# Adding the experts' results into x2 in place, with more weight tiles in rotation

## The chip, the core and the metric

The kernel runs on one core of a Trainium2 chip. The core has a matmul engine (TensorE, PE), a vector engine (VectorE, DVE), an activation engine (ScalarE, ACT), GpSimd (POOL) and SyncE (SP), which here only issues DMAs; 16 DMA engines move the data between DRAM and the on-chip memory (SBUF). Matmul results land in PSUM. The metric is the device time of one execution in microseconds (us); lower is better.

## What is computed

One decoder layer on 256 tokens of 2048 values, in float32. A mixer (pooling, sparse attention and cross-attention, gated) is projected by `w_o` and added to the input; the result is called x2 here. Behind it comes a mixture of experts (MoE) in which each token goes to two experts of one group of four:

```python
x = x + merged @ w_o
x = x + hierarchical_moe(rms_norm(x, g_ffn), ...)   # returned

def hierarchical_moe(h, ...):
    g_top = argmax(h @ w_router_group)               # one of 4 groups
    pe_top, e_local = top_k(softmax(le of g_top), 2) # 2 of its 4 experts
    a = einsum('bsd,edf->bsef', h, w_e_gate)         # 16 experts, 2048 x 512
    b = einsum('bsd,edf->bsef', h, w_e_up)
    act = silu(a) * b * combine[..., None]
    return einsum('bsef,efd->bsd', act, w_e_down)    # 512 x 2048
```

## The kernel before

The layer runs as one stream of matmuls. Up to about 620 us come the projections and the attention; from there to about 717 us the projection by `w_o`, in four chunks of 512 columns (n = 0 to 3), whose results DVE adds into x2 (L817, L820), an SBUF tile of 128 x 2 x 2048; then the routing; and from 731 us the MoE. In the projections every weight tile (`rawt`) is split into a high and a low part: ACT makes `wh` (L114), DVE the product of the difference, `wl` (L115), and PE multiplies with both (L268 to L270).

The MoE gathers its tokens with matmuls. For a group of four experts a 0/1 matrix `sel` says which token stands in which of the 64 places of each expert; `Gather.step` multiplies it with columns of x2 that `part` has split into high and low (ACT L915, DVE L916), and so fills `xg`. The group's four experts run as two pairs, 8 pairs in all. A pair takes 24 weight tiles of 1 MB: 8 for the gate, 8 for the up projection (matmuls `gu<-..,xg`) and 8 for the down projection (`dn<-..,aT`). `scatter` splits the down result into high and low (`ob`, ACT L1107, DVE L1108) and brings it back to token order by a matmul with the transposed `sel` (`selT`); DVE adds that to y (L1115), which for the first pair means x2 + result. In the last pair the rows go out by DMAs on ACT's queue (L1117). A loop behind the 8 pairs repeats them for experts with more than 64 tokens; with these inputs it runs zero times.

All weight tiles are loaded on SP's queue, in program order (`load`, L190). Their SBUF buffers come from what is dead by then, in the order of the deque `order`: 4 buffers of the first normed input (`hq`, tile name `wh`), NEX from a pool of their own (`ex`, `we`), 4 of the raw weights (`raw`, `wr`), and 4 of the merged mixer output (`mx0`, `mx1`, `wm`). `prefetch` takes the next tile of `todo` and the next buffer of `order`, and puts the buffer back at the end, except mx1: these two serve once and then become the accumulators y. Eighteen tiles are prefetched during the `w_o` phase (L733 ff., `pre`, and the `while` after it), and two more, `late`, are loaded after the routing's first part into buffers of a pool that is closed after the first pair. After that a tile is loaded as soon as the buffer that is next in `order` has been read for the last time, so 16 buffers rotate.

`wrt` holds the router's weights, 256 KB. It is loaded early by GpSimd (L356), scaled by DVE (L419) and read in the `w_o` phase (L800); then its memory holds the routing's intermediate tables. GpSimd's other DMAs bring x, biases (`bgt`) and small tables.

Of the kernel before, what the change touches and what calls it, by code (L numbers as in the profile page):

```python
# [20 lines left out]
P = 128  # L21
# [9 lines left out]
CAP = 64  # L31
NEX = 6
LOOK = 2
# [20 lines left out]
def layer_kernel(tc, x, xT, memT, pos, cst, band, gains, bgate, wmem, wxq, widx, wkqvp, wpg, wgb, wo, wr, we, out):  # L54
# [15 lines left out]
    def close(cm):  # L70
        cm.__exit__(None, None, None)

    c_c, cp = pool("const")
    c_raw, raw = pool("raw", bufs=4)
# [55 lines left out]
    big = cp.tile([P, NT, D], F32, tag="big", name="xin")  # L130
    wrt = cp.tile([P, KD, 32], F32, name="wrt")

    xin = big.rearrange("p t d -> p (t d)").rearrange("p (k s) -> p k s", s=S)
# [221 lines left out]

    tc.keep_in_program_order(nc.gpsimd.dma_start(wrt, wr))  # L356
    vm = tok(c4("vm"))
# [45 lines left out]
    def prep_tables():  # L403
        yield
        yield
        yield from tables(tabs)
        for nm, gi, sc in (("q", 0, scale), ("k", 1, 1.0)):
            if sc != 1.0:
                V.tensor_scalar(gn[:, gi], gn[:, gi], sc, None, op0=ALU.mult)
            g1 = gn[:, gi, 0:64].unsqueeze(1).to_broadcast([P, NT, 64])  # L410
            g2 = gn[:, gi, 64:128].unsqueeze(1).to_broadcast([P, NT, 64])
            tl = []
            for tt, (src, g) in enumerate((("cos", g1), ("sin", g2), ("cos", g2), ("sin", g1))):
                d = ap.tile([P, NT, 64], F32, name="tab%s%d" % (nm, tt))
                V.tensor_mul(d, tabs[src], g)
                tl.append(d)
            tabs[nm] = tl
            yield
        tc.keep_in_program_order(V.tensor_mul(wrt, wrt, cs[:, C_GFFN : C_GFFN + KD].unsqueeze(2).to_broadcast([P, KD, 32])))  # L419
        V.tensor_mul(gx, gn[:, 2], gn[:, 3])  # L420
        V.tensor_scalar(gx, gx, scale, None, op0=ALU.mult)
# [307 lines left out]
    todo = deque(use)  # L729
    late = [(0, 7), (0, 15)]  # L730
    for w in late:
        todo.remove(w)

    def prefetch():
        pr, i = todo.popleft()
        kind = order.popleft()
        if kind == "raw":
            w = raw.tile([P, 4, 512], F32, tag="raw", name="wr")
        elif kind == "hq":
            w = htp.tile([P, 4, 512], F32, tag="hq", name="wh")  # L740
        elif kind == "ex":
            w = pools["exp"][1].tile([P, 4, 512], F32, tag="ew", name="we")
        else:
            w = mgp.tile([P, 4, 512], F32, tag=kind, name="wm", bufs=2)
        if kind != "mx1":
            order.append(kind)
        if (pr, i) == (NE // 2 - 1, 23):
            load(w[:, 0:2], we[pr, i, :, 0:2])
            load(w[:, 2:4], we[pr, i, :, 2:4])
        else:  # L750
            load(w, we[pr, i])
        ahead.append(w)
# [29 lines left out]
    for t in range(NT):  # L782
        nc.gpsimd.dma_start(x2[:, t], x[t * P : (t + 1) * P, :])
    ss2 = cp.tile([P, NT, 4], F32, name="ss2")
    rps = sm_tile([P, S], "rps")
    rl_ = []

    def route_in(n, t, ac):
        owp = pools["ow"][1]
        sl = x2[:, t, n * 512 : (n + 1) * 512]  # L790
        ps = sm_tile([P, 4, P])
        for kk in range(4):
            nc.tensor.transpose(ps[:, kk], sl[:, kk * P : (kk + 1) * P], ident)
        xt = owp.tile([P, 4, P], F32, tag="xt", name="xt", bufs=2)
        A.activation(xt, ps, AF.Copy)
        A.activation(ac, sl, AF.Square, accum_out=ss2[:, t, n : n + 1])
        yield

        for kk in range(4):
            mm(rps[32 * kk : 32 * kk + 32, t * P : (t + 1) * P], wrt[:, 4 * n + kk], xt[:, kk],  # L800
               start=n == 0 and t == 0, stop=n == 2 and t == 1)
        yield
        if n == 2 and t == 1:
            lgT = owp.tile([P, 4, P], F32, tag="xt", name="lgT", bufs=2).rearrange("p a b -> p (a b)")[:, :S]
            V.tensor_copy(lgT, rps)
            yield
            rl_.append(sm_tile([P, NT, 20], "rl"))
            for u in range(NT):
                mm(rl_[0][:, u], lgT[:, u * P : (u + 1) * P], cs[:, C_SUM : C_SUM + 20], start=u == 0, stop=False)
            yield  # L810

    last = []
    for n in range(4):
# [9 lines left out]
        def pre(i, n=n):  # L823
            if n == 0 and i == 2:
                drain()
                close(c_cr)
                close(c_bt)
                pools["exp"] = pool("exp", bufs=NEX, side="left")
                pools["ow"] = pool("ow", side="right")
            if i % 2 == 1 and len(ahead) < 4 + NEX:  # L830
                prefetch()
# [29 lines left out]
    for t in range(NT):  # L861
        for kk in range(4):
            pe(rl[:, t], xts[t][:, kk], wrt[:, 12 + kk, 0:20], start=False, stop=t == 1 and kk == 3)
    for t in range(NT):
        pin(A.activation(last[t], x2[:, t, 3 * 512 :], AF.Square, accum_out=ss2[:, t, 3:4]))
    warm(14, ident, P, wps)
    close(pools["ow"][0])
    close(c_spl)
# [4 lines left out]
    pools["x"] = pool("early", side="right")  # L873
    for j, w in enumerate(late):
        et = pools["x"][1].tile([P, 4, 512], F32, name="we%d" % j)
        load(et, we[w])
        ahead.insert(use.index(w), et)

# [18 lines left out]
    C = [P, NT * 5, 4, 4]  # L897
    w = wrt.rearrange("p a b -> p (a b)")
    Rc = w[:, 0:40].rearrange("p (t e) -> p t e", e=4)
# [6 lines left out]

    def part(k, dve=False):

        xs = wk.tile([P, 2, NT, P], F32R, tag="xs", name="xs", bufs=3)
        src = x2[:, :, k * P : (k + 1) * P]  # L910
        if dve:
            pin(V.tensor_copy(xs[:, 0], src))
            pin(V.tensor_sub(xs[:, 1], src, xs[:, 0]))
        else:
            A.activation(xs[:, 0], src, AF.Copy)  # L915
            V.tensor_sub(xs[:, 1], src, xs[:, 0])  # L916
        return xs

    parts0 = [part(k, True) for k in range(3)]
    pin(V.tensor_copy(Rc, R.rearrange("p t g e -> p (t g) e")))  # L920
# [20 lines left out]
    class Gather:  # L941

        def __init__(self, q, slot_, parts=()):
            self.q = q
            self.sel = wk.tile([P, NT, EQ, 64], F32R, tag="sel", name="sel")
            for t in range(NT):
# [5 lines left out]
            self.flat = self.sel.rearrange("p t e s -> p t (e s)")  # L954
            self.xg = None
            self.parts = deque(parts)
# [3 lines left out]
        def split(self, n):  # L960
            while len(self.parts) < n and self.next < KD:
                self.parts.append(part(self.next))
                self.next += 1
# [17 lines left out]
        def back(self, wp):  # L981

            self.selT = wp.tile([P, 2, S], F32R, tag="selT", name="selT", bufs=2)
            ps = sm_tile([P, 2, NT, P])
# [19 lines left out]
    gf = cs[:, C_GFFN : C_GFFN + KD]  # L1004
    ga = Gather(0, slot, parts0)
    ga.step()
# [20 lines left out]

    cwf = rt([P, NT, 18], "cwf")
    cw = wk.tile([P, 2, NT, 18], F32R, name="cw")
# [4 lines left out]

    ys_ = []
    open_ = deque()
# [4 lines left out]

    def pair(pr, slot_, base, store, ga):
        hf = pr % 2
# [27 lines left out]
        else:  # L1071
# [4 lines left out]
            if hf == 0:  # L1076
                ga.factors()
            elif not store:
                nx = Gather(pr // 2 + 1, slot_)
                nx.split(3)  # L1080
# [19 lines left out]
        if nx is not ga:  # L1100
            nx.step()
        if not ys_:
            ys_.extend(mgp.tile([P, D], F32, tag="mx1", name="y", bufs=2) for _ in range(NT))

        def scatter(ad, c0, n):
            ob = w2.tile([P, 2, 512], F32R, tag="ob", name="ob", bufs=2)[:, :, :n]
            A.activation(ob[:, 0], ad, AF.Copy)  # L1107
            V.tensor_sub(ob[:, 1], ad, ob[:, 0])  # L1108
            yield
            for t in range(NT):  # L1110
                ps = sm_tile([P, 512])[:, :n]
                for u in range(2):
                    pe(ps, ga.selT[:, hf, t * P : (t + 1) * P], ob[:, u], start=u == 0, stop=u == 1)
                ys = ys_[t][:, c0 : c0 + n]
                V.tensor_add(ys, base(t)[:, c0 : c0 + n], ps)  # L1115
                if store:
# [41 lines left out]

    yb = lambda t: ys_[t]
    xb = lambda t: x2[:, t]  # L1160
    for pr in range(NE // 2):
        ga = pair(pr, slot, xb if pr == 0 else yb, pr == NE // 2 - 1, ga)
        if pr == 0:
            nri = rounds()


    reg = nc.values_load(nri[0:1, 0:1], min_val=0, max_val=S // CAP - 1)
    todo.extend(use)
    with tc.For_i(0, reg):
        V.tensor_scalar(slot, slot, -float(CAP), None, op0=ALU.add)  # L1170
        ga = Gather(0, slot)
        for pr in range(NE // 2):
            ga = pair(pr, slot, yb, pr == NE // 2 - 1, ga)

# [7 lines left out]
    close(c_raw)  # L1182
    close(c_c)


# [77 lines left out]
```

## Time and profile before

| | us |
|---|---|
| Median of 3 runs (lowest, highest) | 1191.76 (1190.85, 1193.13) |
| Profiled execution | 1192.13 |
| its span | 1190.4 |
| PE busy | 1150.9 |
| DVE busy | 575.2 |
| ACT busy | 424.6 |

The span is what the profile covers of the profiled execution; 1.7 us lie around it. The busy time of an engine is a sum over all stages, so a high share of it does not tell by itself what sets the end: that is read from stretches of the time line, from what an instruction waited for, and from the share in which the DMA engines moved data. HBM reads are 337 MB in all, 201 MB of which are the experts' weights.

### The profile page before, as it was taken

How to read it: one execution, taken by the hardware profiler on the slowest of the kernel's cores; microseconds unless marked ns; L12 is line 12 of the kernel's file. 1: busy time of each engine (PE TensorE's matmuls, PEld its weight loads, DVE VectorE, ACT ScalarE, POOL GpSimd, SP SyncE). 2: the span in 40 equal slices, each digit the busy share in tenths (PEclk: the TensorE clock that was granted, in tenths of full speed). 3: DMA queues.
4: the chain of work that ended last, by engine and by line, in shares of the span. 5: the costliest groups of instructions: out<-in, count | busy, mean ns of one | idle time of the engine just before them, and what ended most of it. 6: DMA issues, size and time to landing. Idle time of an engine off the chain costs nothing.

```text
span 1190.4 us, 14757 instructions
## 1 busy us (share of the span) xinstructions
PE 1150.9 (97%) x5879; PEld 789.1 (66%) x5879; DVE 575.2 (48%) x945; ACT 424.6 (36%) x661; POOL 30.2 (3%) x33
## 2 busy tenths in 40 slices
PE   8999999999999999999999998899999999899976
PEld 5788887888878888888887775454543634363423
DVE  7877468956455465465464444222321512050202
ACT  7765564446544444444444432201100301020000
POOL 4200000000000000000000000000000000000000
PEclk9999999999999999999999999999999999999998
DMA  9646545555546556565787567989999999999996
GB/s 385 208 140 234 184 150 177 177 177 181 202 177 200 206 191 213 189 206 210 252 348 300 188 226 280 384 297 426 426 426 426 427 425 426 426 426 426 426 426 244
DMA packets 49901, 340.34 MB, mean 286 GB/s; under 512 B 5664, under 2 KB 6304, under 8 KB 10400
## 3 DMA queue, kind: packets, MB, share of 16 engines
q1 hardware_dynamic: 46512, 329.83, 71.5%
q0 software_dynamic: 1728, 7.15, 1.7%
q10 hardware_dynamic: 1584, 2.34, 0.6%
q8 instruction: 48, 0.79, 0.3%
q14 instruction: 29, 0.24, 0.1%
HBM read 337.20 MB, written 2.10 MB: 285 GB/s over the span
## 4 chain that ended last, share of the span: by engine, by line


## 5 line engine op out<-in xcount | busy, mean ns | idle before, releaser
L115 DVE TENSOR_TENSOR wl<-rawt,wh 128x1024 fp32r<-128x1024 f32 (+1 forms) x240 | 292.3, 1220 | 212.7 <-ACT wh L114 211.8
L114 ACT ACTIVATE wh<-rawt 128x1024 fp32r<-128x1024 f32 (+1 forms) x240 | 251.0, 1048 | 298.3 <-PE acc L270 292.8
L269 PE MATMUL acc<-wl,hT 128*128 128x512 f32 (+1 forms) x640 | 249.7, 390 | 0.7 <-DVE wl L115 0.7
L270 PE MATMUL acc<-wh,hT 128*128 128x512 f32 (+1 forms) x640 | 247.3, 387 | 0.0
L268 PE MATMUL acc<-wh,hT 128*128 128x512 f32 (+1 forms) x640 | 228.5, 390 | 0.0
L269 PEld LDWEIGHTS acc<-wl,hT 128*128 128x128 f32 x640 | 120.2, 188 | 25.1 <-DVE wl L115 1.1
L270 PEld LDWEIGHTS acc<-wh,hT 128*128 128x128 f32 x640 | 120.2, 188 | 23.2
L268 PEld LDWEIGHTS acc<-wh,hT 128*128 128x128 f32 x640 | 119.2, 188 | 23.4 <-issue 0.3
L842 PE MATMUL gu<-we,xg 128*64 128x512 f32 x400 | 89.8, 596 | 1.5 <-DMA we<-in_we_dram 1.5
L842 PEld LDWEIGHTS gu<-we,xg 128*64 128x64 f32 x400 | 27.3, 137 | 54.2 <-issue 46.6
L842 PE MATMUL gu<-wh,xg 128*64 128x512 f32 x256 | 58.0, 596 | 4.4 <-DMA wh<-in_we_dram 4.4
L915 ACT ACTIVATE xs<-x 128x256 fp32r<-128x256 f32 x61 | 25.2, 416 | 97.4 <-PE sm L842 95.6
L1107 ACT ACTIVATE ob<-dn 128x512 fp32r<-128x512 f32 (+1 forms) x33 | 19.3, 585 | 111.8 <-PE dn L842 111.8
L842 PE MATMUL gu<-wr,xg 128*64 128x512 f32 x240 | 56.2, 596 | 3.0 <-DMA wr<-in_we_dram 3.0
L1108 DVE TENSOR_TENSOR ob<-dn,ob 128x512 fp32r<-128x512 f32 (+1 forms) x33 | 22.3, 676 | 68.7 <-ACT ob L1107 68.7
L1092 DVE SCALAR_TENSOR_TENSOR sgm<-sgm,fac,gu 128x512 f32<-128x512 f32 x8 | 6.0, 747 | 97.2 <-PE gu L842 97.1
L269 PE MATMUL acc<-wl,mgT 128*128 128x512 f32 x128 | 51.3, 401 | 0.0
L1115 DVE TENSOR_TENSOR y<-y,sm 128x512 f32<-128x512 f32 (+1 forms) x58 | 36.3, 665 | 30.5 <-PE sm L842 30.5
L270 PE MATMUL acc<-wh,mgT 128*128 128x512 f32 x128 | 50.7, 396 | 0.0
L268 PE MATMUL acc<-wh,mgT 128*128 128x512 f32 x128 | 46.7, 398 | 0.0
L842 PE MATMUL dn<-we,aT 128*64 128x256 f32 x384 | 46.1, 385 | 0.7 <-ACT aT L1099 0.7
L842 PEld LDWEIGHTS gu<-wh,xg 128*64 128x64 f32 x256 | 17.5, 137 | 42.5 <-issue 30.3
(343 smaller groups left out, 1320.1 us busy)
## 6 DMA issues: line engine op xcount, KB each, us to landing
we<-in_we_dram SPq DMA_DIRECT2D x74, 1024.0 KB, 19.5
rawt<-in_wgb_dram SPq DMA_DIRECT2D x64, 1024.0 KB, 4.8
wh<-in_we_dram SPq DMA_DIRECT2D x48, 1024.0 KB, 19.5
wr<-in_we_dram SPq DMA_DIRECT2D x45, 1024.0 KB, 19.4
rawt<-in_wkqvp_dram SPq DMA_DIRECT2D x24, 1024.0 KB, 4.9
wm<-in_we_dram SPq DMA_DIRECT2D x24, 1024.0 KB, 19.4
rawt<-in_wo_dram SPq DMA_DIRECT2D x16, 1024.0 KB, 4.8
rawt<-in_wmem_dram SPq DMA_DIRECT2D x7, 1024.0 KB, 8.3
```

Of the source, the lines that this page charges most:

```text
L114: pin(A.activation(hi, ps, AF.Copy))
L115: pin(V.tensor_sub(lo, ps, hi))
L268: mm(o, hi[:, c], wh[:, kk], start=f, stop=False)
L269: mm(o, hi[:, c], wl[:, kk], start=False, stop=False)
L270: mm(o, lo[:, c], wh[:, kk], start=False, stop=l)
L842: i = mm(*a, **k)
L915: A.activation(xs[:, 0], src, AF.Copy)
L1092: V.scalar_tensor_tensor(sg, sg, c1s, au, op0=ALU.mult, op1=ALU.mult)
L1107: A.activation(ob[:, 0], ad, AF.Copy)
L1108: V.tensor_sub(ob[:, 1], ad, ob[:, 0])
L1115: V.tensor_add(ys, base(t)[:, c0 : c0 + n], ps)
```

## The change

The experts' results are no longer collected in y. Each pair's results are added into x2 itself. A token belongs to one group only, so for the other groups' gathers an added row is not needed; the adds bring zeros to the rows of other groups. For the overflow loop, which gathers the original values again, x2 is stored to DRAM (`x0d`) before the MoE and would be read back there.

That frees mx1's two buffers, which now rotate. The router's weights get memory of a pool that lives only in the `w_o` phase, are loaded there and scaled there; the routing's tables lie in the not yet filled end of `xg`. selT and ob have one buffer instead of two, and the memory set aside for the descriptors of GpSimd's DMAs is 1024 (`dynamic_dma_scratch_size`). NEX is 9 instead of 6, and one tile is late instead of two: 21 buffers rotate instead of 16, and 22 tiles instead of 20 are issued before the MoE begins to give buffers back.

```diff
-NEX = 6
+NEX = 9
@@ layer_kernel
+    c_d, dp = pool("dram", space=bass.MemoryType.DRAM)
-    wrt = cp.tile([P, KD, 32], F32, name="wrt")
-    tc.keep_in_program_order(nc.gpsimd.dma_start(wrt, wr))
-        tc.keep_in_program_order(V.tensor_mul(wrt, wrt, cs[:, C_GFFN : C_GFFN + KD].unsqueeze(2).to_broadcast([P, KD, 32])))
@@ weight tiles
-    late = [(0, 7), (0, 15)]
-    for w in late:
-        todo.remove(w)
+    late = (0, 15)
+    todo.remove(late)
-        if kind != "mx1":
-            order.append(kind)
+        order.append(kind)
@@ pre(i), n == 0 and i == 2
+                wrt_.append(pools["ow"][1].tile([P, KD, 32], F32, name="wrt"))
+                nc.gpsimd.dma_start(wrt_[0], wr)
+                V.tensor_mul(wrt_[0], wrt_[0], cs[:, C_GFFN : C_GFFN + KD].unsqueeze(2).to_broadcast([P, KD, 32]))
@@ after the last add into x2
+    for t in range(NT):
+        load(x0d[t], x2[:, t])
-    for j, w in enumerate(late):
-        et = pools["x"][1].tile([P, 4, 512], F32, name="we%d" % j)
-        load(et, we[w])
-        ahead.insert(use.index(w), et)
+    et = pools["x"][1].tile([P, 4, 512], F32, name="we15")
+    load(et, we[late])
+    ahead.insert(use.index(late), et)
-    w = wrt.rearrange("p a b -> p (a b)")
+    xg0 = wk.tile([P, KD, 256], F32, tag="xg", name="xg")
+    w = xg0[:, 14:16].rearrange("p a b -> p (a b)")
@@ back, scatter
-            self.selT = wp.tile([P, 2, S], F32R, tag="selT", name="selT", bufs=2)
+            self.selT = wp.tile([P, 2, S], F32R, tag="selT", name="selT")
-            ob = w2.tile([P, 2, 512], F32R, tag="ob", name="ob", bufs=2)[:, :, :n]
+            ob = w2.tile([P, 2, 512], F32R, tag="ob", name="ob")[:, :, :n]
-                ys = ys_[t][:, c0 : c0 + n]
-                V.tensor_add(ys, base(t)[:, c0 : c0 + n], ps)
+                ys = x2[:, t, c0 : c0 + n]
+                V.tensor_add(ys, ys, ps)
@@ build
-    nc = _bacc.Bacc("TRN2", target_bir_lowering=False, num_devices=1)
+    nc = _bacc.Bacc("TRN2", target_bir_lowering=False, num_devices=1, dynamic_dma_scratch_size=1024)
```

On SP's queue, from the last tile prefetched in the `w_o` phase on, before (we_5626 and we_5628 are the late tiles, the four `wh` the first reissues):

```order
L190 DMA wm<-in_we_dram 128x2048
L190 DMA we_5626<-in_we_dram 128x2048
L190 DMA we_5628<-in_we_dram 128x2048
L190 DMA wh<-in_we_dram 128x2048 x4
L190 DMA we<-in_we_dram 128x2048 x6
L190 DMA wr<-in_we_dram 128x2048
L190 DMA wm<-in_we_dram 128x2048
L190 DMA wr<-in_we_dram 128x2048
L190 DMA wm<-in_we_dram 128x2048
L190 DMA wr<-in_we_dram 128x2048 x2
L190 DMA wh<-in_we_dram 128x2048 x4
```

The same place after:

```order
L190 DMA wm<-in_we_dram 128x2048
L190 DMA x0d<-x_4891 128x2048 x2
L190 DMA we_5637<-in_we_dram 128x2048
L190 DMA wh<-in_we_dram 128x2048 x4
L190 DMA we<-in_we_dram 128x2048 x9
L190 DMA wr<-in_we_dram 128x2048
L190 DMA wm<-in_we_dram 128x2048
L190 DMA wr<-in_we_dram 128x2048
L190 DMA wm<-in_we_dram 128x2048
L190 DMA wr<-in_we_dram 128x2048
```

The two stores of x2 stand where a late tile stood, and a round of the rotation has 21 tiles instead of 16.

On DVE, at the start of the `w_o` phase (sg is the gated mixer, wl the low part of a `w_o` tile), before:

```order
L773 TENSOR_TENSOR sg<-acc,sg 128x512 x2
L775 TENSOR_TENSOR sg<-sg 128x512 x2
L115 TENSOR_TENSOR wl<-rawt,wh 128x1024 x3
L115 TENSOR_TENSOR mgT_2930<-sm,mgT_2930 128x4x128 x2
L115 TENSOR_TENSOR wl<-rawt,wh 128x1024 x4
```

and after:

```order
L769 TENSOR_TENSOR sg<-acc,sg 128x512 x2
L771 TENSOR_TENSOR sg<-sg 128x512 x2
L116 TENSOR_TENSOR wl<-rawt,wh 128x1024
L830 TENSOR_TENSOR wrt<-wrt,cs 128x512
L116 TENSOR_TENSOR wl<-rawt,wh 128x1024 x2
L116 TENSOR_TENSOR mgT_2929<-sm,mgT_2929 128x4x128 x2
```

The scaling of wrt, which before stood far ahead, now stands between two of the wl products.

## Rows read from the trace of the kernel before

**Rows 1.** The page, busy us and share of each engine.

```profile
PE 1150.9 (97%) x5879; PEld 789.1 (66%) x5879; DVE 575.2 (48%) x945; ACT 424.6 (36%) x661; POOL 30.2 (3%) x33
```

**Rows 2.** The page's 40 slices, DMA engines' busy share in tenths.

```profile
DMA  9646545555546556565787567989999999999996
```

**Rows 3.** Windows: stretch, length, PE, PEld, DVE, ACT, POOL, PE clock, DMA share, GB/s.

```profile
644.00:674.00 30.00, 30.00 (x156) 23.27 (x155) 14.48 (x14) 15.04 (x22) 0.00 (x0) 1.00 0.56 199
720.00:726.00 6.00, 4.89 (x43) 4.70 (x43) 4.74 (x29) 1.16 (x4) 0.44 (x2) 1.00 0.99 377
726.00:735.00 9.00, 7.47 (x44) 4.43 (x45) 5.28 (x25) 3.13 (x7) 0.00 (x0) 1.00 0.26 87
765.00:810.00 45.00, 41.80 (x248) 19.67 (x246) 11.64 (x23) 5.72 (x9) 0.00 (x0) 0.96 0.81 313
840.00:1140.00 300.00, 288.50 (x1686) 134.39 (x1685) 78.99 (x151) 35.28 (x69) 0.00 (x0) 1.00 1.01 426
```

**Rows 4.** PE's time line (start, length), first gate matmuls of pairs 1 to 7.

```profile
791.85 1.94 PE L842 MATMUL gu<-we,xg 128*64 128x512 f32 x8
...
848.43 1.89 PE L842 MATMUL gu<-wr,xg 128*64 128x512 f32 x8
...
898.90 1.89 PE L842 MATMUL gu<-we,xg 128*64 128x512 f32 x8
...
1005.88 1.89 PE L842 MATMUL gu<-we,xg 128*64 128x512 f32 x8
...
1066.75 1.89 PE L842 MATMUL gu<-wr,xg 128*64 128x512 f32 x8
...
1118.52 1.94 PE L842 MATMUL gu<-we,xg 128*64 128x512 f32 x8
```

**Rows 5.** The time line at the end; in brackets idle time before and its releaser.

```profile
1177.38 1.08 PE L842 MATMUL dn<-wm,aT 128*64 128x256 f32 x8 [0.28 <-DMA wm<-in_we_dram]
...
1178.39 1.00 PE L842 MATMUL sm<-ob,selT 128*128 128x256 f32 x5
1178.57 0.38 ACT L1107 ACTIVATE ob<-dn 128x256 fp32r<-128x256 f32 x1 [3.12 <-PE dn L842]
```

**Rows 6.** SP's time line: reissues of weight tiles in the first pair.

```profile
733.19 6.76 SPq L190 DMA_DIRECT2D wh<-in_we_dram  x4
...
763.26 0.33 SPq L190 DMA_DIRECT2D wm<-in_we_dram  x1
775.30 4.37 SPq L190 DMA_DIRECT2D wr<-in_we_dram  x2
...
793.82 5.03 SPq L190 DMA_DIRECT2D we<-in_we_dram  x3
```

**Rows 7.** Landing times: least, median, most of tile wm; medians of GpSimd's loads.

```profile
DMA to landing us min/median/max: 4.7/19.5/20.4
...
bgt<-in_bgate_dram POOLq DMA_DIRECT2D x12, 256.0 KB, 4.1
...
wrt<-in_wr_dram POOLq DMA_DIRECT2D x1, 256.0 KB, 6.2
...
post<-in_pos_dram POOLq DMA_DIRECT2D x1, 1.0 KB, 3.3
```

**Rows 8.** DVE's adds that read x2 in the first pair: ns, first and last start.

```profile
L1115 DVE TENSOR_TENSOR y<-x,sm x8: 679/687/689, 780.0 to 795.1; 128x512 f32<-128x512 f32 x8
```

**Rows 9.** The time line at the start of the `w_o` phase, PE and DVE.

```profile
620.35 0.39 PE L269 MATMUL acc<-wl,crh 128*128 128x512 f32 x1
...
624.90 1.23 DVE L115 TENSOR_TENSOR wl<-rawt,wh 128x1024 fp32r<-128x1024 f32 x1 [0.76 <-ACT wh L114]
...
630.31 0.40 PE L269 MATMUL acc<-wl,mgT 128*128 128x512 f32 x1
```

More of the change, by code (lines that the diff above doesn't have):

```diff
@@ L784, in layer_kernel @@
     ss2 = cp.tile([P, NT, 4], F32, name="ss2")
+    x0d = dp.tile([NT, P, D], F32, name="x0d")
     rps = sm_tile([P, S], "rps")
     rl_ = []
+    wrt_ = []
     def route_in(n, t, ac):
@@ L799, in route_in @@
         for kk in range(4):
-            mm(rps[32 * kk : 32 * kk + 32, t * P : (t + 1) * P], wrt[:, 4 * n + kk], xt[:, kk],
+            mm(rps[32 * kk : 32 * kk + 32, t * P : (t + 1) * P], wrt_[0][:, 4 * n + kk], xt[:, kk],
                start=n == 0 and t == 0, stop=n == 2 and t == 1)
@@ L862, in layer_kernel @@
         for kk in range(4):
-            pe(rl[:, t], xts[t][:, kk], wrt[:, 12 + kk, 0:20], start=False, stop=t == 1 and kk == 3)
+            pe(rl[:, t], xts[t][:, kk], wrt_[0][:, 12 + kk, 0:20], start=False, stop=t == 1 and kk == 3)
     for t in range(NT):
@@ L905, in layer_kernel, with part @@
     SQ = EQ * 64
-    def part(k, dve=False):
+    def part(k, x0=None, dve=False):
         xs = wk.tile([P, 2, NT, P], F32R, tag="xs", name="xs", bufs=3)
[L910 to L913, printed above, removed]
-        else:
-            A.activation(xs[:, 0], src, AF.Copy)
-            V.tensor_sub(xs[:, 1], src, xs[:, 0])
+        c = slice(k * P, (k + 1) * P)
+        if x0 is not None:
+            for t in range(NT):
+                A.activation(xs[:, 0, t], x0[t][:, c], AF.Copy)
+                V.tensor_sub(xs[:, 1, t], x0[t][:, c], xs[:, 0, t])
+        elif dve:
+            pin(V.tensor_copy(xs[:, 0], x2[:, :, c]))
+            pin(V.tensor_sub(xs[:, 1], x2[:, :, c], xs[:, 0]))
+        else:
+            A.activation(xs[:, 0], x2[:, :, c], AF.Copy)
+            V.tensor_sub(xs[:, 1], x2[:, :, c], xs[:, 0])
         return xs
-    parts0 = [part(k, True) for k in range(3)]
+    parts0 = [part(k, dve=True) for k in range(3)]
     pin(V.tensor_copy(Rc, R.rearrange("p t g e -> p (t g) e")))
@@ L941, in layer_kernel, with __init__ @@
     class Gather:
-        def __init__(self, q, slot_, parts=()):
+        def __init__(self, q, slot_, parts=(), xg=None, x0=None):
             self.q = q
+            self.x0 = x0
             self.sel = wk.tile([P, NT, EQ, 64], F32R, tag="sel", name="sel")
@@ L954, in __init__ @@
             self.flat = self.sel.rearrange("p t e s -> p t (e s)")
-            self.xg = None
+            self.xg = xg
             self.parts = deque(parts)
@@ L961, in split @@
             while len(self.parts) < n and self.next < KD:
-                self.parts.append(part(self.next))
+                self.parts.append(part(self.next, self.x0))
                 self.next += 1
@@ L1004, in layer_kernel @@
     gf = cs[:, C_GFFN : C_GFFN + KD]
-    ga = Gather(0, slot, parts0)
+    ga = Gather(0, slot, parts0, xg0)
     ga.step()
@@ L1025, in layer_kernel @@
     V.tensor_mul(cmb, cmb, s2.unsqueeze(2).to_broadcast([P, NT, NE]))
-    cwf = rt([P, NT, 18], "cwf")
+    cwf = w[:, 440:476].rearrange("p (t e) -> p t e", t=NT)
     cw = wk.tile([P, 2, NT, 18], F32R, name="cw")
@@ L1033, in layer_kernel @@
     V.tensor_sub(cw[:, 1], cwf, cw[:, 0])
-    ys_ = []
     open_ = deque()
@@ L1040, in finish, with pair @@
             next(open_.popleft(), None)
-    def pair(pr, slot_, base, store, ga):
+    def pair(pr, slot_, store, ga):
         hf = pr % 2
@@ L1078, in pair @@
             elif not store:
-                nx = Gather(pr // 2 + 1, slot_)
+                nx = Gather(pr // 2 + 1, slot_, x0=ga.x0)
                 nx.split(3)
@@ L1101, in pair @@
             nx.step()
-        if not ys_:
-            ys_.extend(mgp.tile([P, D], F32, tag="mx1", name="y", bufs=2) for _ in range(NT))
         def scatter(ad, c0, n):
-            ob = w2.tile([P, 2, 512], F32R, tag="ob", name="ob", bufs=2)[:, :, :n]
+            ob = w2.tile([P, 2, 512], F32R, tag="ob", name="ob")[:, :, :n]
             A.activation(ob[:, 0], ad, AF.Copy)
@@ L1157, in rounds @@
         return nri
-    yb = lambda t: ys_[t]
-    xb = lambda t: x2[:, t]
     for pr in range(NE // 2):
-        ga = pair(pr, slot, xb if pr == 0 else yb, pr == NE // 2 - 1, ga)
+        ga = pair(pr, slot, pr == NE // 2 - 1, ga)
         if pr == 0:
@@ L1168, in layer_kernel @@
     todo.extend(use)
+    rest = [k for k in order if k != "mx1"]
+    order.clear()
+    order.extend(rest)
     with tc.For_i(0, reg):
+        x0 = [mgp.tile([P, D], F32, tag="mx1", name="x0", bufs=2) for _ in range(NT)]
+        for t in range(NT):
+            load(x0[t], x0d[t])
         V.tensor_scalar(slot, slot, -float(CAP), None, op0=ALU.add)
-        ga = Gather(0, slot)
+        ga = Gather(0, slot, x0=x0)
         for pr in range(NE // 2):
-            ga = pair(pr, slot, yb, pr == NE // 2 - 1, ga)
+            ga = pair(pr, slot, pr == NE // 2 - 1, ga)
     close(pools["w2"][0])
@@ L1183, in layer_kernel @@
     close(c_c)
+    close(c_d)
 def _consts():
```

## Prediction, made before the changed kernel was timed

> **What bounds the kernel now.** The page's first part gives TensorE (PE) 97% of the span [rows 1]; alone that would make it the bound from end to end. The page's 40 slices say otherwise: the DMA row stands at 4 to 7 through slice 20 and at 9 from slice 28 to slice 39 [rows 2]. So I cut the span by windows. From 840 to 1140 us the 16 DMA engines are busy for 1.01 of the time, at 426 GB/s [rows 3]. This is the MoE, which streams 192 weight tiles of 1 MB once. A tile of 1.0486 MB costs 1.0486/426 = 2.46 us there, and the 24 tiles of a pair of experts 59.1 us.
>
> PE needs less than that. Two pairs without long waits take, from the first row of one to that of the next, 56.6 us (odd: 791.85 to 848.43) and 50.5 us (even: 848.43 to 898.90). Near the end they take longer: the odd pair from 1005.88 60.9, the even one from 1066.75 51.8, and the last, from 1118.52 to about 1180.4, 61.9 [rows 4]. Against 56.6, 50.5 and (no next gather to make) 50.5 that is 4.3 + 1.3 + 11.4 = 17 us in which PE waited for weights. The last such wait stands at 1177.38, where the down-projection's matmuls stood for a DMA [rows 5]. **The bound is the DMA stream from the first reissue at 733.19 to the last tile**; PE comes second, 17 us behind.
>
> So I ask what the stream carries after 733.19, and where it stands still. Of 192 tiles 20 are issued before that, which leaves 172. It stands still in two places. Ahead of 733 it runs dry: the windows show a DMA share of 0.99 for 720 to 726 and 0.26 for 726 to 735 [rows 3], so what was asked for before had landed by about 728.4. And after 765: SyncE's (SP's) queue shows 14 issues from 733.19 to 763.26, then nothing until 775.30 [rows 6]. SP sends in program order, and its next tile needs the buffer of the first down-projection tile. From 765 to 810 the stream moved 313 GB/s [rows 3]; against 426 the loss is 45 x 113/426 = 11.9 us.
>
> **The change part by part.** *Three more tiles before the routing, one late tile fewer.* By the first reissue 22 tiles are issued instead of 20, so 170 are left: 2 x 2.46 = **-4.9 us** of stream. The three added loads stand among the wo loads at about 645 to 663 us, where the DMA share is 0.56 [rows 3]: 7.4 us of work in 13 idle ones of those 30. They cost nothing; without that cover they would cost up to 7.4.
>
> *21 buffers in rotation instead of 16.* Before, 16 of the 20 tiles lay in buffers that come back: 14 gate/up tiles, and of the next four only every other one, since the two mx1 buffers became accumulators. After, 15 gate/up buffers come back (one tile is late), then every down buffer. Fifteen reissues start at 733.19. The shortest landing of a 1 MB tile is 4.7 us [rows 7], of which 2.46 is moving, so bytes flow 2.2 us after an issue, from 735.4. They last 15 x 2.46 = 36.9, to 772.3. The next buffer is free at 775.30, as before, so bytes flow again at 777.5: a gap of 5.2. From there nine buffers (eight down tiles and the next pair's first) come free by 793.82 [rows 6], one in 2.1 us on average, faster than 2.46, so no further gap opens. The loss of 11.9 becomes 5.2: **-6.7 us**. Bounds: 0 if the gap stays, -11.9 if it goes altogether.
>
> *The store of x0d.* Two stores of 1 MB go to DRAM through SP's queue, ahead of the late tile and of the first reissues. No row shows a write of that size. At a tile's price they are 4.9 us, and one late tile of 2.46 is gone: 728.4 - 2.5 + 4.9 = 730.8, inside the idle stretch that ends at 735.4. At twice the price they end at 735.7, and a push of the stream by less than 5.2 is given back by the gap at 772. I take **0**; bounds 0 and +4.9 (neither stretch takes them). The first add into x2 at 780.0 [rows 8] must wait until the store has read; 45 us lie between.
>
> On the tile's price the Trainium skill, "DMA: Bandwidth & Descriptors", section "Where 436 GB/s comes from", says that the HBM side, about 358 GB/s, binds transfers between HBM and SBUF. By that (an estimate) a tile would cost 2.93 us, the first term would be -5.9 and the whole 1180.0. The trace shows 426 GB/s over 300 us [rows 3], so the measurement decides.
>
> *wrt loaded at about 620 us instead of early.* GpSimd's load now waits for PE's last read of a cross-attention tile, at 620.35 + 0.39 = 620.7, and VectorE (DVE) multiplies wrt, in program order, just ahead of the wl product that before began at 624.90 after 0.76 of idling, so at 624.1 [rows 9]. The load took 6.2 us [rows 7] and lands at 626.9; the multiply, 0.69 as the adds of its shape [rows 8], ends at 627.6, the wl product, 1.23 long, at 628.8. The matmuls that read it start at 630.31 [rows 9]. So the cover is 1.5 us: **0**. Once it is gone, every us is a us of PE. Bounds: -0.6 (0.25 MB leave the busy start of the kernel) and +2.
>
> *In-place adds.* As many and as long as before, 0.69 us each [rows 8]. In even pairs three splits of x2 for the next gather now stand between the first two scatters on DVE, each no longer than such an add, 2.1 us at most; DVE is busy for 79 of 300 us there [rows 3]. I take 0, bounds 0 and +0.5.
>
> *One ob buffer instead of two.* At the very end ACT writes the second half's ob at 1178.57 while PE still multiplies with the first half's, from 1178.39. Four of those five matmuls of 1.00 us must end first, at about 1179.2 [rows 5]: **+0.6**, on the path. Bounds 0 and +1. Elsewhere a whole down chunk lies between two scatters, so one buffer does. The one selT buffer is written by a step that stands behind its readers in PE's order anyway: 0.
>
> *Smaller descriptor memory for GpSimd's DMAs.* I take 0, with a rival below.
>
> **Sum:** -4.9 - 6.7 + 0.6 = -11.0 us. Against the profiled execution, 1192.13 (span 1190.4 and 1.7 around it), that gives 1181.1; this execution lies 0.4 over the median of 1191.76, from which it is 1180.8. I take **1181.0**. PE allows it: its 17 us of waiting shrink to about 6.
>
> **The rivals.** *The whole gap closes.* If the stream meets a buffer whenever it wants one, all 11.9 go: 1191.8 - 4.9 - 11.9 + 0.6 = 1175.6. For it: a late store fills the gap with bytes that were due earlier. Against it: the first down buffer can't be free before its matmuls, which hang on DVE and ACT work that the change leaves alone. Chance 0.13.
>
> *Only the two tiles count.* If the reissues are held up elsewhere (the stores ahead of them in the queue, or the eight transfers that the program keeps in flight), the gap stays: 1191.8 - 4.9 + 0.6 = 1187.5. For it: no row shows the write. Against it: even at twice a tile's price the stores fit to 0.3 us. Chance 0.16.
>
> *PE is the bound already,* as its 97% say; then looking further ahead moves only the tail: 1192.4. Against it: the 17 us of waiting for weights. Chance 0.04.
>
> *GpSimd's load starts late.* If it can't be issued while DVE works, it starts when DVE comes to stand for it, at 624.1 instead of 620.7, 3.4 late, less 1.5 of cover: +1.9, 1182.9. Against it: twelve loads of wrt's size, issued between 104 and 557 us by the same engine, landed in 4.1 us in the median [rows 7], no later than wrt. This is the Trainium skill's rule in "SBUF — State Buffer", section "Summary: rules for kernel authors": descriptor generation for GpSimd's DMAs starves while DVE runs in its 2x and 4x modes; whether DVE does so at 620 no row here shows. Chance 0.04.
>
> *wrt comes in pieces,* the one that ends slower. If the smaller descriptor memory cuts GpSimd's load into pieces that wait for one another, DVE stands, all later wl products behind it, and PE with it. A piece costs at least what the smallest such load took, 3.3 us [rows 7]. Eight pieces: 26.4 instead of 6.2, 20.2 late, less 1.5 of cover: +18.7, 1199.7. It turns slower than before from a landing after 18.7 us (6.2 + 1.5 + 11.0), six pieces. For it: the memory is cut and no row shows what it holds; against it: wrt is a quarter of the largest loads on that path. Chance 0.06.
>
> **How the numbers follow.** The forecast has 0.56, with 1178.5 to 1183.5 as its own range (a gap between 2.7 and 7.7). The rivals have 0.13, 0.16, 0.04, 0.04 and 0.06; 0.01 is left for what I don't see. The range 1175.0 to 1188.0 takes in the forecast, the closed gap, the two tiles alone and the late start; it leaves out the rest, 0.11, and the far ends of those cases. A measurement of this kernel tells about 0.2%, 2.4 us, from no change. Faster 0.89; same 0.05; slower 0.06.
>
> **What would show it.** After the change: 15 issues on SP's queue from about 733.2, the next at about 775.3; a DMA share near 1 from 735 to 772, a gap of about 5 us, then 426 GB/s to the end; no long waits for weights until the last two pairs, the last at about 1166; the tail's second ob waiting for PE; DVE waiting some 2.8 us for wrt at 624, PE not waiting at 630. I am wrong if PE waits near 630, if the stores are still moving past 741, or if 765 to 810 still lose over 8 us.

## The result, and the profile after

| | before | after |
|---|---|---|
| Median, us (lowest, highest, runs) | 1191.74 (1190.85, 1193.13, 4) | 1183.87 (1183.02, 1185.69, 4) |
| Profiled execution | 1192.13 | 1183.17 |
| its span | 1190.4 | 1181.4 |

The ratio is 0.9934, with a 95% interval of 0.9920 to 0.9948: 7.9 us faster, inside the range, where 11 was forecast; it lies 0.4 us above the forecast's own range of 1178.5 to 1183.5. The same program run again later gave a median of 1185.15 beside 1191.84, 6.7 us faster, so the gain is 7 to 8 us.

The windows of the changed kernel, with the columns of [rows 3]:

```profile
726.00:735.00 9.00, 6.77 (x43) 4.23 (x43) 5.96 (x30) 3.13 (x7) 0.00 (x0) 1.00 0.69 269
...
765.00:810.00 45.00, 41.80 (x242) 19.70 (x243) 13.02 (x31) 7.27 (x12) 0.00 (x0) 0.92 0.91 372
...
840.00:1140.00 300.00, 293.85 (x1728) 139.29 (x1724) 79.86 (x152) 34.81 (x69) 0.00 (x0) 1.00 1.01 426
```

The idle stretch of 726 to 735 now carries the stores (0.69 for 0.26). From 765 to 810 the stream moves 372 GB/s for 313, so its loss is 45 x 54/426 = 5.7 us for 11.9. Behind that it moves 426 as before: still the bound, though PE's waits for weights behind 850 us add up to 3.7 us only, for 11.1 before. SP's time line shows why the loss is not smaller; it answers [rows 6]:

```profile
719.01 0.86 SPq L190 DMA_DIRECT2D x0d<-x  x2
722.43 0.33 SPq L190 DMA_DIRECT2D we<-in_we_dram  x1
733.90 6.78 SPq L190 DMA_DIRECT2D wh<-in_we_dram  x4
743.36 19.23 SPq L190 DMA_DIRECT2D we<-in_we_dram  x9
763.99 0.33 SPq L190 DMA_DIRECT2D wr<-in_we_dram  x1
766.84 0.33 SPq L190 DMA_DIRECT2D wm<-in_we_dram  x1
777.11 0.33 SPq L190 DMA_DIRECT2D wr<-in_we_dram  x1
```

Fifteen reissues up to 766.84, as forecast, and the first down buffer's at 777.11 instead of 775.30. It comes 1.8 us later: 0.7 because the first reissue does (733.90 for 733.19), 1.1 because of what PE and DVE do in between. PE's and DVE's time line there, with the window of the granted clock:

```profile
770.00:775.00 5.00, 2.70 (x12) 1.72 (x14) 1.43 (x2) 0.60 (x1) 0.00 (x0) 0.63 0.82 344
...
768.45 0.66 PE L848 MATMUL sm<-ident,sel 128*128 128x128 f32 x4
769.14 0.76 DVE L958 TENSOR_TENSOR sel<-cs,slot 128x256 fp32r<-128x256 f32 x2 [3.38 <-PE sm L848]
...
769.93 0.75 DVE L1093 SCALAR_TENSOR_TENSOR sgm<-gu,fac,sgm 128x512 f32<-128x512 f32 x1
770.72 0.75 DVE L1100 SCALAR_TENSOR_TENSOR sgm<-sgm,fac,gu 128x512 f32<-128x512 f32 x1
...
771.62 1.09 PE L848 MATMUL sm<-ident,sgm 128*128 128x128 f32 x4 [2.51 <-DVE sgm L1100]
...
773.39 3.68 PE L843 MATMUL dn<-wr,aT 128*64 128x256 f32 x16 [0.69 <-ACT aT L1107]
```

DVE stands for 3.38 us ahead of sel, the selection matrix of the next group, which may be written only when PE has transposed the old one. The two sgm operations, for which PE waits, stand behind it in DVE's order. PE idles 2.51 us, its granted clock falls to half (0.63 in 770 to 775), and the first down tile takes 3.68 us where a tile at the full clock takes 1.95. Before, the same wait stood there with a shorter fall (0.79):

```profile
770.00:775.00 5.00, 3.42 (x20) 2.13 (x22) 0.75 (x1) 0.60 (x1) 0.00 (x0) 0.79 0.16 67
...
770.89 0.63 PE L847 MATMUL sm<-ident,sgm 128*128 128x128 f32 x4 [2.51 <-DVE sgm L1092]
772.21 3.06 PE L842 MATMUL dn<-wr,aT 128*64 128x256 f32 x16 [0.69 <-ACT aT L1099]
```

The tail, which answers [rows 5]:

```profile
1163.44 1.95 PE L843 MATMUL dn<-wh,aT 128*64 128x256 f32 x16 [0.47 <-DMA wh<-in_we_dram]
...
1166.55 0.38 ACT L1113 ACTIVATE ob<-dn 128x256 fp32r<-128x256 f32 x1 [2.87 <-PE sm L843]
...
1167.76 1.95 PE L843 MATMUL dn<-wh,aT 128*64 128x256 f32 x16 [1.25 <-DVE ob L1114]
...
1170.42 0.38 ACT L1113 ACTIVATE ob<-dn 128x256 fp32r<-128x256 f32 x1 [3.48 <-PE sm L843]
...
1170.85 1.09 PE L843 MATMUL sm<-ob,selT 128*128 128x256 f32 x4 [0.47 <-ACT ob L1113]
```

The single ob is waited for twice: at 1166.55 by the first half's ob, behind which the last weight matmuls stand (1.25 us), and at 1170.42 by the second half's. The last wait of PE for weights stands at 1163.44, for 1177.38 before. The 13.9 us between the two are not the gain: before, PE waited there for the second half of the very last tile, now for the tile ahead of it, and the last tile's matmuls wait for ob instead.

wrt, which answers [rows 9]:

```profile
628.80 0.69 DVE L830 TENSOR_TENSOR wrt<-wrt,cs 128x512 f32<-128x512 f32 x1 [3.98 <-DMA wrt<-in_wr_dram]
629.40 2.36 DVE L116 TENSOR_TENSOR wl<-rawt,wh 128x1024 fp32r<-128x1024 f32 x2
...
631.00 0.40 PE L269 MATMUL acc<-wl,mgT 128*128 128x512 f32 x1
```

DVE waits 4.0 us for it, the first wl product behind it ends at about 630.6, and the matmul that needs it, at 631.00, doesn't wait. The cover held, with 0.4 us to spare.

### The profile page after: what moved, and what is told of

Read it like the earlier page. It is cut to its first block, busy times and chain, and to the rows that moved or that the text cites. A ratio compares the mean times of both kernels' runs of the same rounds, so it can differ in the third digit from the quotient of the medians.

```text
span 1181.4 us, 14749 instructions
## 1 busy us (share of the span) xinstructions
PE 1146.8 (97%) x5879; PEld 790.6 (67%) x5879; DVE 574.8 (49%) x945; ACT 423.5 (36%) x661; POOL 30.1 (3%) x33
## 4 chain that ended last, share of the span: by engine, by line
## 5 line engine op out<-in xcount | busy, mean ns | idle before, releaser
L843 PE MATMUL gu<-we,xg 128*64 128x512 f32 x464 | 103.3, 594 | 2.2 <-DMA we<-in_we_dram 2.2
L843 PEld LDWEIGHTS gu<-we,xg 128*64 128x64 f32 x464 | 32.3, 137 | 64.6 <-issue 56.9
L1123 DVE TENSOR_TENSOR x<-x,sm 128x512 f32<-128x512 f32 (+1 forms) x66 | 41.3, 668 | 38.2 <-PE sm L843 38.2
L843 PE MATMUL gu<-wh,xg 128*64 128x512 f32 x200 | 44.7, 595 | 0.0
L843 PE MATMUL gu<-wm,xg 128*64 128x512 f32 x184 | 43.5, 594 | 0.5 <-DMA wm<-in_we_dram 0.5
L1092 ACT ACTIVATE sgm<-gu,fac 128x512 f32<-128x512 f32 x8 | 5.5, 687 | 105.1 <-PE gu L843 58.3
```

Source lines behind the costliest of these rows:

```text
L843: i = mm(*a, **k)
L1092: A.activation(sg, ag, AF.Sigmoid, scale=r2s)
L1123: V.tensor_add(ys, ys, ps)
```

## The experiments

Each kernel was timed in several runs beside runs of the kernel before on the same chip; those had medians of 1192.1, 1191.8 and 1191.8 in the three groups of four.

**The next group's sel behind the first pair's sgm** (`sel_late`). Only the order on DVE differs; sel and sgm are now kept in program order:

```diff
-                pin(V.tensor_tensor(self.sel[:, t], ...
+                tc.keep_in_program_order(V.tensor_tensor(self.sel[:, t], ...
-        V.scalar_tensor_tensor(sg, ag, r2s, sg, ...)
+        tc.keep_in_program_order(V.scalar_tensor_tensor(sg, ag, r2s, sg, ...))
-        V.scalar_tensor_tensor(sg, sg, c1s, au, ...)
+        tc.keep_in_program_order(V.scalar_tensor_tensor(sg, sg, c1s, au, ...))
```

> The changed kernel, but DVE builds the next group's sel in program order, behind the first pair's two sgm operations instead of ahead of them. Theory: the loss that is left between 765 and 810 us (5.7 us) is set by the release of the first down tile's buffer. In the changed kernel sgm stands behind sel, which waits for PE's transposes until 769.14, though ACT's sigmoid was done at 767.5; PE then idles from 769 to 771.6, its granted clock falls, and the first down tile takes 3.7 us. With sgm first the transposes of sgm start some 2.0 us earlier, and with the clock up the release at 777.1 comes some 3.5 us earlier: 2.0 to 3.5 us faster than the changed kernel's 1183.9, so 1180.4 to 1181.9. Rival (the loss comes from the two stores or the eight transfers in flight): no change, 1183.9.

Measured: 1180.33. PE's time line of the place, and SP's:

```profile
770.61 0.66 PE L848 MATMUL sm<-ident,sgm 128*128 128x128 f32 x4 [0.27 <-DVE sgm L1100]
771.95 1.95 PE L843 MATMUL dn<-wr,aT 128*64 128x256 f32 x16 [0.69 <-ACT aT L1107]
```

```profile
735.15 6.77 SPq L190 DMA_DIRECT2D wh<-in_we_dram  x4
...
768.09 0.33 SPq L190 DMA_DIRECT2D wm<-in_we_dram  x1
773.94 0.33 SPq L190 DMA_DIRECT2D wr<-in_we_dram  x1
```

The release comes 38.8 us behind the first reissue instead of 43.2, and 765 to 810 moves 412 GB/s, which leaves 1.5 us of the loss. So the gap that was left is set by the first down buffer, as the sum had it.

**Three copies of x2 instead of one** (`store_3x`; the DRAM tile and its reader, not shown, grow to match).

```diff
-    for t in range(NT):
-        load(x0d[t], x2[:, t])
+    for r in range(3):
+        for t in range(NT):
+            load(x0d[r, t], x2[:, t])
```

> The changed kernel with x0d stored three times, 6 MB instead of 2. Theory: the stores fill an idle stretch and push the stream into the gap at 772, which gives it back. Added work 4 x 1.0486 MB at 426 GB/s = 9.8 us; cover is (1 - 0.69) x 9 = 2.8 us of idle DMA from 726 to 735, 1.1 to the first reissue's bytes, and 5.7 of gap: 9.6. So 0 to +1 us, 1183.9 to 1184.9. Rival (stores are paid in full, two of them 4.9 us of the changed kernel's time): +9.8, 1193.7.

Measured: 1184.35, 0.5 over the changed kernel's first median and 0.8 under its second. Its windows:

```profile
726.00:735.00 9.00, 6.94 (x43) 4.25 (x43) 5.80 (x29) 3.14 (x7) 0.00 (x0) 1.00 1.00 423
735.00:765.00 30.00, 30.00 (x156) 13.55 (x156) 7.33 (x17) 3.76 (x9) 0.00 (x0) 1.00 1.01 426
765.00:810.00 45.00, 41.80 (x254) 19.33 (x252) 13.24 (x30) 7.28 (x12) 0.00 (x0) 1.00 1.01 426
```

The DMA engines never stand still and the time is the same: the added 9.8 us fill the idle stretch and the gap. In this profile PE's clock stayed up and the release came at 774.76, 2.4 us earlier than in the changed kernel's, which makes the gap easier to fill; the medians take in both cases. A write costs about what a read does (423 GB/s with both).

**No copy at all** (`no_store`; the two lines are taken out).

> The changed kernel without the two stores of x0d (left out: the copy that the overflow rounds, which do not run here, would read). Theory: the stores end at about 730, ahead of the first reissue's bytes at 736, so they cost nothing: 1183.9, within 0.7. Rival (stores are paid in part): up to 4.9 faster, 1179.0.

Measured: 1184.48, beside 1185.15 for the changed kernel in the same group. The DMA share of 726 to 735 is 0.23 again. The two intervals overlap (0.9912 to 0.9946, 0.9922 to 0.9953): nothing gained that can be told. The two profiles agree within 0.2 us in the first reissue and the release, and their spans are 1183.2 and 1184.0, so a cost of up to 0.8 us is not excluded.

**In place, but with as many tiles ahead as before** (`inplace_16buf`).

```diff
-NEX = 9
+NEX = 6
...
-    late = (0, 15)
+    late = [(0, 7), (0, 15)]
...
```

> One part alone: the results are added in place, mx1's two buffers rotate, x0d is stored, wrt is loaded late, ob and selT are single; but NEX is 6 and two tiles are late, as before. So 18 buffers rotate and 20 tiles are issued before the first reissue, as in the kernel before. Theory of the prediction: 172 tiles are left, two more than in the changed kernel, and one reissue fewer before the gap: 14 tiles end at 770.6, bytes flow again 2.2 us behind the release at 777.1, and 158 tiles follow against 155: +7.4 us over the changed kernel, 1191.3; a release as early as before's 775.3 would give 1189.5. Rival (the rotation of mx1 is the gain and the look ahead brings nothing): as the changed kernel, 1183.9.

Measured: 1191.03 (interval 0.9978 to 1.0002). In-place adds with mx1 rotating, 18 buffers, bring 1.1 us, by the interval between nothing and 2.6; the look ahead that the freed memory buys brings the rest. The profiled execution took 1189.29: there the clock stayed up and the release stands at 776.10, between the theory's two cases, so part of the agreement of the median with 1191.3 is luck of the executions.

**The tail's ob in dead buffers** (`tail_ob`).

```diff
+            if n == 256:
+                ob = wk.tile([P, 2, NT, P], F32R, tag="xs", ...).rearrange("p u t q -> p u (t q)")
+            else:
                 ob = w2.tile([P, 2, 512], F32R, tag="ob", name="ob")[:, :, :n]
```

> The changed kernel, but the two halves of the last down chunk put their high and low parts into two buffers of xs, which is dead by then, instead of both into the single ob. Theory: the single ob costs twice in the tail, once where the first half's ob waits for the scatter before it and PE's last weight matmuls wait for that ob (1.25 us at 1167.76), once where the second half's ob waits for the first half's scatter: 1.2 us faster than the changed kernel, 1182.7. By the prediction's term only the second counts: 0.6 faster, 1183.3. Rival: the tail is set by the weights' landing and the stores of the output, 0.

Measured: 1181.83. The last weight matmuls now follow at once; from the last wait for weights (1162.48) to the end of the span it is 16.9 us, where the changed kernel has 18.0:

```profile
1162.48 1.95 PE L843 MATMUL dn<-wh,aT 128*64 128x256 f32 x16 [0.46 <-DMA wh<-in_we_dram]
...
1165.48 1.95 PE L843 MATMUL dn<-wh,aT 128*64 128x256 f32 x16
...
1166.26 0.71 PEld L843 LDWEIGHTS dn<-wh,aT 128*64 128x64 f32 x8 [0.15 <-DMA wh<-in_we_dram]
```

So the single ob costs 1.05 us, not 0.6. The second half of the last tile is waited for again (1166.26), and from there to the end it is 13.1 us, as in the kernel before from 1177.38 (13.0). The other 1.0 of the 2.0 is no gain of this edit: in this profile the clock fell for a shorter time, and the release came 42.2 us behind the first reissue for 43.2.

**The changed kernel again** (`changed_again`, no edit).

> The changed kernel itself again, to see what differs between executions of one program: 1183.9 by the runs so far. In its first profile PE's granted clock fell to 0.63 from 770 to 775 us; in a profile with three stores it stayed at 1.00 with the same instructions there. If that fall is by chance, the release of the first down buffer lies between 774.7 and 777.1 and the time between 1182 and 1185; if it belongs to the program, it lies at 777 again.

Measured: 1185.15. The first down tile took 3.68 us again, and the release lay 43.1 us behind the first reissue. But the first reissue itself stood at 735.32, 1.4 us later than in the first profile. That belongs to the first 100 us, which the prediction had not looked at. PE's time line there, before:

```profile
51.23 0.40 PE L270 MATMUL acc<-wh,memT 128*128 128x512 f32 x1
51.55 0.64 PE L170 MATMUL ssT<-sqa,ones 128*32 128x256 f32 x8
```

and after:

```profile
49.93 0.64 PE L170 MATMUL ssT<-sqa,ones 128*32 128x256 f32 x8 [0.97 <-POOL sqa L164]
50.50 0.74 PE L268 MATMUL acc<-wh,memT 128*128 128x512 f32 x2
52.54 0.50 PE L269 MATMUL acc<-wl,memT 128*128 128x512 f32 x1 [1.30 <-DVE wl L116]
```

With wrt's load gone from GpSimd's queue the scheduler put ssT, a sum of squares that GpSimd prepares (sqa), 11 matmul rows earlier on PE, and there PE waits for GpSimd, and behind it 1.30 us for DVE.

Both profiles of the program have these waits; what differs behind them is PE's granted clock. The window in the first profile and in this one:

```profile
50.00:55.00 5.00, 3.70 (x21) 2.39 (x22) 5.00 (x8) 1.85 (x2) 1.21 (x2) 1.00 0.48 128
...
50.00:55.00 5.00, 3.69 (x17) 2.35 (x12) 5.00 (x8) 1.77 (x2) 1.13 (x2) 0.80 0.50 136
```

The first bias load of GpSimd, at 105.43 and 106.87, shows that the 1.4 us are there by then.

**wrt early again** (`wrt_early`: a tile of its own, load and scaling where they were; NEX 8 to make room).

> The changed kernel with wrt in a tile of its own from the start, loaded and scaled where it was before; for its 2 KB per partition NEX is 8, so 20 buffers rotate and 21 tiles are issued before the MoE gives buffers back. Theory: one tile more is left for the stream, +2.5 us; DVE's wait of 4.0 us at 624 goes, which is worth nothing; and the second ssT matmul of the first 100 us, which PE reached 2.6 us earlier after the change and there waited for GpSimd, stands where it stood before, -0.7: 1185.6, with the first bias load behind it at about 104.7 us instead of 105.4. Rival (wrt's late load costs PE time): 1183 or less.

Measured: 1184.37, with one tile more to stream after 733 than the changed kernel's 1185.15 in the same group. Its first reissue stands at 733.41, 1.9 us ahead of the changed kernel's in that group. The time lies between the 1185.6 of the theory and the 1183 of the rival, and its interval (0.9918 to 0.9955) reaches both; that PE did not wait for wrt is read from the changed kernel's trace.

**Only the early order** (`early_order`).

```diff
+    dmy = scr.tile([P, KD, 32], F32, tag="dmy", name="dmy", bufs=1)
+    tc.keep_in_program_order(nc.gpsimd.dma_start(dmy, wr))
     vm = tok(c4("vm"))
```

> The changed kernel with a 256 KB load on GpSimd's queue where wrt's load stood before (into a tile that nothing reads), which puts the second ssT matmul of the first 100 us back behind the next weight matmuls on PE; wrt itself is still loaded late. Theory: the first bias load then starts at about 104.8 us as in the kernel before, against 105.4 to 106.9 in the profiles of the changed kernel and its variants, and everything behind it moves with it: 0.7 to 2.0 us faster than the changed kernel's 1185.1 of the last batch, 1183.1 to 1184.4. Rival (the first 100 us differ by chance, not by the order): 1185.

Measured: 1181.63, with runs from 1179.6 to 1185.5: 1.5 us under the range of the theory, and with an interval (0.9890 to 0.9931) that overlaps the changed kernel's. So what the order costs is read from the trace, not from this time. ssT stands without a wait again:

```profile
51.63 0.64 PE L170 MATMUL ssT<-sqa,ones 128*32 128x256 f32 x8
```

The marker that I had named, the first bias load, was the wrong one: it started at 107.56. The first reissue stands at 733.34. Over all profiles that is the clean sign: 733.19 to 733.41 in the five with the old order, 733.75 to 735.33 in the nine with the new one. These nine fall into two groups by PE's granted clock from 50 to 55 us (table below): where it stays at 1.00 the first reissue stands at 733.75 to 733.91, where it falls to 0.69 to 0.80 at 735.10 to 735.33. With the old order it stays at 1.00 in all five. Against the kernel before, the new order costs 0.6 to 0.7 us, and 1.9 to 2.1 where the clock falls.

**PE kept busy in the first pair** (`pe_kept_busy`).

```diff
+        if pr == 0:
+            warm(18, ident, P, sm_tile([P, 512]))
         ps = sm_tile([P, 4, P])
```

> The changed kernel with 18 matmuls without use on PE, in the first pair between the transposes of sel and those of sgm, where PE idles for 2.5 us. The order on DVE is as in the changed kernel. Theory: the granted clock then does not fall to half, the first down tile takes 1.95 us instead of up to 3.68, and the release behind 777 to 778 comes 1.0 to 2.0 us earlier; the stream with it: 1183.1 to 1184.1 against 1185.1. Rival (only the waiting for DVE counts, the clock does not): 1185, or later by what the added matmuls hold up.

Measured: 1183.04. Counted from the first reissue, PE comes to the transposes of sgm 1.3 us later than it did after the wait (39.05 us for 37.72), yet the release comes earlier, 42.3 us behind the first reissue:

```profile
768.79 4.18 PE L282 MATMUL sm<-ident 128*128 128x128 f32 x36
772.81 0.60 PE L848 MATMUL sm<-ident,sgm 128*128 128x128 f32 x4
774.09 1.95 PE L843 MATMUL dn<-wr,aT 128*64 128x256 f32 x16 [0.69 <-ACT aT L1109]
```

**The kernel before with sel behind sgm** (`before_sel_late`, the diff of `sel_late` on the kernel before).

> The kernel before, with the next group's sel behind the first pair's sgm on DVE and nothing else. Theory: there too the stream stands until the first down buffer is released, 42.1 us behind the first reissue; with sgm first it is 38.8 as in sel_late's profile: 3.3 us faster than before, 1188.5. So this gain is not the change's. Rival (before, the losses behind 780 set the time): less than 1 us, 1191.

Measured: 1188.46 (interval 0.9954 to 0.9980); the release comes 38.8 us behind the first reissue:

```profile
733.22 6.77 SPq L190 DMA_DIRECT2D wh<-in_we_dram  x4
...
772.01 3.78 SPq L190 DMA_DIRECT2D wr<-in_we_dram  x2
```

**The fixes together** (`both_fixes`: `sel_late` and `tail_ob`; `three_fixes`: with `early_order` too).

> The changed kernel with both of the changes that helped: the next group's sel behind the first pair's sgm on DVE, and the last two halves' ob in buffers of xs. Theory: the two gains lie in different places, so they add: 3.5 + 1.05 (from the profiles of the two runs), 1179.3. Rival (with the stream's gap gone PE or the output stores set the end): 1180.3, as with the first alone.

> The version with both fixes, and the load of early_order. Theory: it adds, 0.7 to 2.0 below 1178.5: 1176.5 to 1177.8. Rival: 1178.5.

Measured: 1178.51 (0.9881, interval 0.9859 to 0.9902) and 1177.53 (0.9875, interval 0.9856 to 0.9894): the second 14.2 us under the kernel before, and both faster than either kernel of this study. The 1.0 between the two lies within their intervals.

The place of the release in every profile (first reissue; first down buffer's reissue behind it; length of the first down tile on PE; PE's granted clock from 50 to 55 us):

| kernel | first reissue | behind it | first down tile | clock at 50 to 55 |
|---|---|---|---|---|
| before | 733.19 | 42.1 | 3.06 | 1.00 |
| before_sel_late | 733.22 | 38.8 | 1.95 | 1.00 |
| changed | 733.90 | 43.2 | 3.68 | 1.00 |
| changed_again | 735.32 | 43.1 | 3.68 | 0.80 |
| no_store | 735.33 | 43.2 | 3.68 | 0.76 |
| early_order | 733.34 | 43.2 | 3.68 | 1.00 |
| wrt_early | 733.41 | 42.5 | 3.40 | 1.00 |
| tail_ob | 733.91 | 42.2 | 3.15 | 1.00 |
| store_3x | 733.75 | 41.0 | 1.95 | 1.00 |
| inplace_16buf | 735.10 | 41.0 | 1.95 | 0.69 |
| pe_kept_busy | 733.76 | 42.3 | 1.95 | 1.00 |
| sel_late | 735.15 | 38.8 | 1.95 | 0.71 |
| both_fixes | 735.21 | 38.8 | 1.95 | 0.71 |
| three_fixes | 733.33 | 38.8 | 1.95 | 1.00 |

## Why the prediction came out as it did

The direction, the mechanism and the range were right; the forecast of 1181.0 lies 2.9 us under the first median and 4.2 under the second, which both lie above the forecast's own 1178.5 to 1183.5 (the whole range reaches up to 1188.0 for the rival of the two tiles). What the sum had too small all lies on one side, so nothing cancelled. Point by point:

- **What bounds it.** Right: the stream. But the 17 us in which PE waited for weights were read from the lengths of pairs; what the trace lists as PE's waits for weights behind 850 us is 11.1, barely more than the 11.0 that the forecast takes off, and 3.7 are left after the change. (And the DMA row's first slice is a 9, not a 4 to 7; nothing rests on it.)
- **Two tiles fewer in the stream, -4.9.** Right. The 426 GB/s stand in every profile from 840 to 1140, so a tile costs 2.46 us; `inplace_16buf`, which undoes the look ahead, with one reissue fewer before the gap, came out at 1191.03 for 1191.3. The 358 GB/s of the Trainium skill's page ("DMA: Bandwidth & Descriptors", "Where 436 GB/s comes from") were not the limit here: 426 GB/s reading, and 423 with the stores of `store_3x` among the loads.
- **The gap, 11.9 to 5.2.** Right in its mechanism: 15 reissues, a gap, then no more. It measured 5.7. The step that failed in size is "the next buffer is free at 775.30, as before": with the first reissue set aside, it came 1.1 us later, since PE's clock fell further (3.68 us for 3.06 in the first down tile, the rest in the transposes ahead of it, 1.09 for 0.63). 5.2 and 1.1 would make 6.3; the 0.6 between that and the 5.7 of the window are not placed. I had called the stretch work that the change leaves alone; its instructions are, its clock is not.
- **The stores, 0.** Right within what can be told, from both sides: leaving them out gains 0.7 us with intervals that overlap, three times as many cost nothing. The rival that only the two tiles count falls with the loss of 5.7 where it has 11.9.
- **wrt, 0.** Right, with less cover than I had: the load was issued at 621.83, 1.1 us later than the 620.7 of the forecast (0.7 because this whole stretch lies later), landed in 6.9 us for 6.2, and DVE waited 4.0 us for 2.8. PE did not wait. So neither of the rivals on wrt came; with 0.4 us left, the cover was nearly gone. The smaller descriptor memory did not slow larger loads either: the two 1 MB loads of x by GpSimd landed in 6.0 us in the median, as before.
- **One ob buffer, +0.6.** Too small: 1.05, by the profile of `tail_ob`. I had looked at the second half's ob alone. The first half's waits too, for the scatter before it, and PE's last weight matmuls write the other half of the PSUM tile that this ob reads, so they wait with it.
- **Not in the sum: the first 100 us, +0.6 to +2.1.** I gave the early load's removal a bound of -0.6 for its bytes and did not ask whether taking an instruction off GpSimd's queue moves others. It moved ssT on PE. That the order is the cause is shown by `early_order` and `wrt_early`; whether it costs 0.6 or 2.1 us goes with PE's granted clock from 50 to 55 us, which falls behind the new waits in five of nine profiles. Why it falls in one execution and not in another is open.

With these the first profile adds up: -4.9 - 6.7 + 0.7 + 1.1 + 1.05 = -8.8, where its span fell by 9.0. The second, with 2.1 in place of 0.7 and 1.0 for 1.1, gives -7.5, where the span fell by 6.4. Of the 1.1 between them, 0.6 lie behind the last wait for weights (18.55 us to the end of the span for 17.96); the rest is not placed.

The rival that the whole gap closes asked for an earlier release. It comes with `sel_late`, which leaves 1.5 us of the loss, and the change does not bring it; `before_sel_late` shows that this gain, 3.3 us, was to be had without the change.

## What to carry to other kernels

When a stream of transfers is the bound, count what it still has to carry from the moment buffers begin to come back, and find the one release at which it runs dry; memory is worth a tile's time per buffer ahead, and a transfer that fits into an idle stretch ahead of that release cost nothing here that could be told. Then ask what sets that release: here an operation that nobody waits for yet stood ahead of one that PE waits for, in one engine's order. And where a scheduler sets the order, look at the order of the whole program after an edit, also at places that the edit does not name: removing one load cost up to 2 us in a stage 600 us ahead of the work that was changed.

## What the runs showed of the chip

The granted clock after a stall was not the same from execution to execution. With the same instructions and the same 2.51 us of idling on PE, the first down tile took 1.95 us in two profiles (granted clock 1.00 from 770 to 775), 3.06 to 3.40 in three and 3.68 in four, which is the lower of the two levels (1.2 for 2.4 GHz) nearly throughout. It moves the release by 2.2 us (41.0 to 43.2), and the stream's end with it. The same holds 700 us earlier: behind the waits of 0.97 and 1.30 us of the new order, the clock from 50 to 55 us was 1.00 in four profiles and 0.69 to 0.80 in five, and the first reissue came 1.2 to 1.6 us later in these. With PE kept busy, or its wait shortened to 0.27 us, the tile took 1.95 us in every profile. The time of a run goes with its mean clock: of the changed kernel's ten runs, those at 0.994 took 1183.0 to 1183.7 us, those at 0.990 and 0.991 1184.6 to 1185.9.
